# A transformer layer on one core: the second residual, its norm and the Gelu tiles' buffers rebuilt

## The chip, the cores and the metric

One core of one Trainium2 chip runs the whole program in one launch. The time is the device time of the run in microseconds (us). Engines are named as the profile names them: PE is TensorE (matmuls; PEld its weight loads), DVE VectorE, ACT ScalarE, POOL GpSimd, SP SyncE. SP, ACT and POOL also issue DMAs, each into a queue of its own, and every engine works through its own instructions in order.

## The reference

One layer on 512 tokens of width 2048, all in float32: two attention branches, a layer norm, and a PEER block, a retrieval of experts of which 16 out of 16384 are chosen in each of 8 heads. The change touches what stands around PEER:

```
y   = (sigmoid(gate_a) * ya + sigmoid(gate_b) * yb) @ w_o
x   = layer_norm(alpha * x + g1 * y, ln1_g, ln1_b)          # LN1
h2  = x * (1 + sc2) + sh2
p   = peer(h2, ...)
x   = layer_norm(alpha * x + g2 * p, ln2_g, ln2_b)          # the end

def peer: for each token t and head h
    q = h2 @ wq;  top 16 of the scores -> 16 experts e, gates gt
    a = <h2, u_tab[e]>;  w = gt * gelu(a);  p += w * v_tab[e]
```

## The kernel before

**Two ways through PEER.** 352 of the 512 tokens (TD) go the dense way: all 16384 experts are multiplied, as 128 tiles of 128 experts, in 32 groups of four (GE). A u product (u_mm, 96 matmuls of 352 columns) gives a Gelu tile; the tile is multiplied by its gates (weigh), split into a high and a low half (W_0h, W_0l and so on), and goes as moving operand into the v product (v_mm, four blocks of 12 matmuls of 352 columns). The sums of the v products are kept transposed in SBUF, in accT. For the other 160 tokens each chosen row of u_tab and v_tab is gathered from memory (320 indirect DMAs, issued by POOL) and used by DVE.

**Weights.** A Stream (L60 to L100) loads pieces of 128x1024 through SP's queue (raw), ACT rounds each to its high half (whi, L91), DVE takes the difference (wlo, L92). A product takes three matmuls: L151, L154, L155 in the helper mm3; L1141 to L1143 in v_mm.

**Stages, as the trace shows them.** To 1105: conditioning and attention. 1105 to 1340: the product with w_o and LN1, whose normalised rows (rx) POOL stores to n_d (L803). 1340 to 1684: queries, scores against the keys (loaded by POOL, L933) and their top 16, and meanwhile the first 23 u products through u_first (L900). 1684 to 2060, the g phase: for each of 11 chunks of 32 tokens the gates are spread into a tile over all experts, by one-hot rows (o, L1076, DVE), scaled ones (og, L1082, ACT) and their product (L1083, PE); ACT stores 2 MB of them to g_d (L1087), and beside it run three more u products and five gathers. 2060 to 3150, the main loop: 18 groups, u product and v product of the group before, by turns, with gathers paced by step(). 3150 to the end: the 14 groups whose Gelu tiles u_first had stored to ga_d come back (L1252) and only v products remain.

**First Gelu tiles.** u_first's tile glf has one buffer, and its store to ga_d is issued by POOL (L904), in whose queue the gathers and the copies that pace them (L288) stand too.

**The end.** step(VW) paces gathers through the first VN = 9 end groups. After that POOL computes alpha*LN1 again from n_d, by mul_add (L1206 multiplies, L1208 adds, on 512 columns at a time), also for the gathered tokens (h2g, accg) and the 32 mixed ones (accx). In group 12 accT is transposed back by PE (L1280), multiplied by the row g2 on DVE (L1240, yt) and added by POOL (L1241). In group 13 the v products are made with tokens on the partitions (v_part, 128x512 results in PSUM banks), and again yt, add and bn_stats (L1243). finish() (L1217) then makes the norm: for some columns by ACT (L1222) and POOL, for others by DVE (L1227), and stores the result.

**What sets the order.** The functions write instructions in program order for each engine; a scheduler then moves them within what the data and the buffers allow. Pinned ones keep their order (SP's loads, wlo).

## Time and profile before

| | us |
|---|---|
| three timed runs | 3712.43, 3717.99 (median), 3718.40 |
| profiled execution | 3710.02 |
| its span | 3708.2 |
| PE busy in it | 3572.1 (96%) |
| DVE, ACT, POOL busy | 2718.9, 1756.2, 1071.9 |
| granted TensorE clock, mean | 0.985 |

Read it in this way: where one engine is busy nearly throughout, the stages in which it is not are looked up (busy time by stretch), then what it waited for there (waits by releaser), then what the releaser itself did at that moment (timeline of that engine). The rows stand below.

### The profile page before, as it was taken

What the parts mean: (1) busy time and instruction counts of PE and PEld (TensorE: products, weight loads), DVE (VectorE), ACT (ScalarE), POOL (GpSimd) and SP (SyncE); (2) the same over time, 40 slices, a digit from 0 to 9 for tenths busy, and PEclk for the clock granted to TensorE, in tenths of its full rate; (3) what the DMA queues carried; (4) which work ended last, traced back from release to release, by engine and by line L of the source; (5) the groups of instructions that cost most, each with busy time, mean ns of one, the idle gap of its engine ahead of it and who ended that gap; (6) DMA issues with size and microseconds to landing.
All of it is one profiled execution on the core that took longest, in us unless ns stands there. A gap on an engine that the chain in (4) does not pass through costs nothing.

```text
span 3708.2 us, 52907 instructions
## 1 busy us (share of the span) xinstructions
PE 3572.1 (96%) x20073; PEld 3287.0 (89%) x20073; DVE 2718.9 (73%) x3735; ACT 1756.2 (47%) x3055; POOL 1071.9 (29%) x1186
## 2 busy tenths in 40 slices
PE   8999999999999999999998899999999999999977
PEld 6888888877778899899988899999999999899976
DVE  8756587445455669988978587777777778788866
ACT  3233332233333555446755355555455555676652
POOL 0001110011110000004434353433344434345474
PEclk9999999999999999999999999999999999999988
DMA  9645588644365665348988799989898999999942
GB/s 397 248 170 216 176 317 303 233 137 133 121 223 182 200 203 172 121 131 292 356 316 339 278 358 347 338 328 349 329 363 329 347 345 347 367 371 368 359 157 84
DMA packets 211024, 996.73 MB, mean 269 GB/s; under 512 B 26624, under 2 KB 26800, under 8 KB 153648
## 3 DMA queue, kind: packets, MB, share of 16 engines
q1 hardware_dynamic: 132048, 526.45, 40.0%
q0 software_dynamic: 75984, 441.58, 31.8%
q10 hardware_dynamic: 2736, 25.32, 1.7%
q8 instruction: 157, 2.57, 0.3%
q14 instruction: 99, 0.81, 0.1%
HBM read 930.42 MB, written 61.51 MB: 267 GB/s over the span
## 4 chain that ended last, share of the span: by engine, by line
PE 80%; issue 5%; DMA 5%; DVE 5%; POOL 2%; ACT 2%; POOLq 0%; SPq 0%; DVEq 0%; ACTq 0%
PE main L155 11%; PE main L151 11%; PE main L154 11%; PE o L1143 8%; PE o L1141 7%; PE o L1142 7%; PE q L151 6%; PE q L155 6%; PE q L154 6%; DMA adaw<-in_w_ada_t 2%; DVE wlo L92 1%; DMA ga_d<-glf 1%; DVE adaw L292 1%; PE g L1083 1%; DMA row<-in_peer_u,gidx 1%
## 5 line engine op out<-in xcount | busy, mean ns | idle before, releaser
L92 DVE TENSOR_TENSOR wlo<-raw,whi 128x1024 fp32r<-128x1024 f32 x800 | 991.7, 1248 | 558.1 <-ACT whi L91 426.6
L91 ACT ACTIVATE whi<-raw 128x1024 fp32r<-128x1024 f32 x800 | 837.8, 1056 | 941.3 <-PE main L154 489.9
L151 PE MATMUL q<-dh,whi 128*128 128x352 f32 x1680 | 549.4, 327 | 25.5 <-ACT glf L903 24.2
L155 PE MATMUL q<-dh,wlo 128*128 128x352 f32 x1680 | 543.6, 324 | 0.9 <-DVE wlo L92 0.9
L154 PE MATMUL q<-dl,whi 128*128 128x352 f32 x1680 | 543.0, 323 | 0.0
L288 POOL COPY row<-wlo 128x1 f32<-128x1 f32 x320 | 186.7, 584 | 748.7 <-DVE row L1035 322.8
L151 PE MATMUL main<-hh,whi 128*128 128x512 f32 x912 | 352.9, 393 | 9.1 <-ACT hh L346 8.8
L1144 ACT ACTIVATE accT<-o 128x352 f32<-128x352 f32 x496 | 223.7, 462 | 282.5 <-PE o L1143 281.5
L154 PE MATMUL main<-hl,whi 128*128 128x512 f32 x912 | 357.0, 391 | 0.0
L155 PE MATMUL main<-hh,wlo 128*128 128x512 f32 x912 | 349.3, 393 | 0.2 <-DVE wlo L92 0.2
L151 PEld LDWEIGHTS q<-dh,whi 128*128 128x128 f32 x1680 | 318.3, 189 | 27.5 <-ACT glf L903 25.6
L155 PEld LDWEIGHTS q<-dh,wlo 128*128 128x128 f32 x1680 | 318.4, 190 | 1.2 <-DVE wlo L92 1.2
L154 PEld LDWEIGHTS q<-dl,whi 128*128 128x128 f32 x1680 | 319.2, 190 | 0.0
L1035 DVE SCALAR_TENSOR_TENSOR row<-row,h2g 128x2048 f32<-128x2048 f32 x128 | 291.7, 2285 | 29.0 <-DMA row<-in_peer_u,gidx 27.9
L1041 DVE SCALAR_TENSOR_TENSOR h2g<-row,au,h2g 128x2048 f32<-128x2048 f32 x127 | 297.9, 2346 | 8.3 <-DMA row<-in_peer_v,gidx 7.9
L292 DVE SCALAR_TENSOR_TENSOR adaw<-adaw,cond 128x2048 f32<-128x2048 f32 x96 | 218.5, 2288 | 103.9 <-DMA adaw<-in_w_ada_t 100.3
L151 PE MATMUL main<-qh,whi 128*128 128x352 f32 (+2 forms) x752 | 242.2, 323 | 1.0 <-ACT whi L91 1.0
L155 PE MATMUL main<-qh,wlo 128*128 128x352 f32 (+2 forms) x752 | 242.8, 324 | 0.0
L154 PE MATMUL main<-ql,whi 128*128 128x352 f32 (+2 forms) x752 | 242.0, 322 | 0.0
L1060 POOL DMA_INDIRECT row<-in_peer_v,gidx x128 | 217.3, 1698 | 46.7 <-POOL row L288 35.3
L1134 ACT ACTIVATE o<-accT 128x352 f32<-128x352 f32 x480 | 219.2, 471 | 7.4
L151 PEld LDWEIGHTS main<-hh,whi 128*128 128x128 f32 x912 | 172.1, 189 | 46.6 <-ACT hh L346 10.7
(1355 smaller groups left out, 8161.3 us busy)
## 6 DMA issues: line engine op xcount, KB each, us to landing
raw<-in_wst SPq DMA_DIRECT2D x288, 512.0 KB, 3.8
raw<-in_u_t SPq DMA_DIRECT2D x256, 512.0 KB, 6.0
raw<-in_v_t SPq DMA_DIRECT2D x256, 512.0 KB, 7.6
adaw<-in_w_ada_t SPq DMA_DIRECT2D x96, 1024.0 KB, 7.0
g_d<-stg ACTq DMA_DIRECT2D x11, 2048.0 KB, 10.9
gt<-g_d POOLq DMA_DIRECT2D x18, 704.0 KB, 10.4
ga_d<-glf POOLq DMA_DIRECT2D x56, 176.0 KB, 4.4
gl<-ga_d POOLq DMA_DIRECT2D x56, 176.0 KB, 7.9
```

Source lines behind the costliest of these rows:

```text
L91: self.nc.scalar.activation(hi, raw, AF.Copy)
L92: self.pin(self.nc.vector.tensor_tensor(out=lo, in0=raw, in1=hi.bitcast(F32), op=ALU.subtract))
L151: op = nc.tensor.matmul(ps, lh, rh, start=first, stop=False)
L154: nc.tensor.matmul(ps, lh, rl, start=False, stop=False)
L155: nc.tensor.matmul(ps, ll, rh, start=False, stop=last)
L292: pin(nc.vector.scalar_tensor_tensor(w, w, 1.0, cond, op0=ALU.mult, op1=ALU.mult, accum_out=mod[:, j : j + 1]))
L1035: op = nc.vector.scalar_tensor_tensor(row, row, 1.0, h_, op0=ALU.mult, op1=ALU.mult, accum_out=a_[:, c : c + 1])
L1041: op = nc.vector.scalar_tensor_tensor(accs[n], row, a_[:, c : c + 1], accs[n], op0=ALU.mult, op1=ALU.add)
L1141: nc.tensor.matmul(o, vh[:, s], wh, start=first, stop=False, **kw)
L1142: nc.tensor.matmul(o, vh[:, s], wl, start=False, stop=False, **kw)
L1143: nc.tensor.matmul(o, vl[:, s], wh, start=False, stop=last_, **kw)
L1144: nc.scalar.activation(sum_, o, AF.Copy)
```

## The change

1. **LN1** (x1_rows): DVE makes alpha*LN1 with its gain and bias at once, 16 chunks of 128x512 in two buffers (xc), two operations each, and POOL stores each chunk to n_d (256 KB). The four 1 MB stores of the bare normalised rows go.
2. **First Gelu tiles**: glf has two buffers; the store to ga_d is issued by ACT instead of POOL.
3. **g2 upstream**: the last group's eight weight pieces are multiplied by g2 on DVE before they are split (Stream.by); accT is scaled by the g2 column when ACT evacuates it in group 12; accx is multiplied once.
4. **Residual and sums in PSUM**: in the last group ACT writes x1 into a bank, PE adds accT by a matmul with the identity (48 in all, in place of 48 transposes) and the mixed tokens by the selection matrix, and the v products accumulate on top. bn_stats and the norm read the bank.
5. **Gathered tokens** (gathered()): on DVE at group 11 instead of POOL.
6. **Pacing**: VN 9 to 11, VW 1.0 to 0.8; four gl buffers instead of two in the end; six matmuls of 160 columns at group 0 write the rest of each bank.
7. **Norm of the three dense token tiles**: per tile DVE takes columns 512 to 2047, ACT and POOL the first 512.

```diff
@@ Stream.fill
+            by = self.by.get(self.plan[i][0])
+            if by is not None:
+                r2 = raw.rearrange("p (a b) -> p a b", a=2)
+                self.nc.vector.tensor_tensor(
+                    out=r2, in0=r2, in1=by.unsqueeze(1).to_broadcast([P, 2, 512]), op=ALU.mult
+                )
@@ LN1
-        for t in tt:
-            nc.gpsimd.dma_start(n1_d[t], rx[t])
+    def x1_rows(pas):
+        for t in (2 * pas, 2 * pas + 1):
+            for c in range(4):
+                cs = slice(c * 512, (c + 1) * 512)
+                xc = rp_.tile([P, 512], F32, tag="xc", name=f"xc{t}{c}", bufs=2)
+                nc.vector.tensor_tensor(out=xc, in0=rx[t][:, cs], in1=l1["ln1_g"][:, cs], op=ALU.mult)
+                nc.vector.tensor_tensor(out=xc, in0=xc, in1=l1["ln1_b"][:, cs], op=ALU.add)
+                nc.gpsimd.dma_start(n1_d[t][:, cs], xc)
@@ u_first
-        gl = wk.tile([P, TD], F32, tag="gl", name=f"glf{e}", bufs=1)
+        gl = wk.tile([P, TD], F32, tag="gl", name=f"glf{e}", bufs=2)
         nc.scalar.activation(gl, ps[:, :TD], AF.Gelu)
-        nc.gpsimd.dma_start(ga_d[e], gl)
+        nc.scalar.dma_start(ga_d[e], gl)
@@ v_mm
-            nc.scalar.activation(sum_, o, AF.Copy)
+            if by is None:
+                nc.scalar.activation(sum_, o, AF.Copy)
+            else:
+                nc.scalar.activation(sum_, o, AF.Copy, scale=by[:, j * 4 + dd : j * 4 + dd + 1])
@@ pacing
-    VW, VN = 1.0, 9
+    VW, VN = 0.8, NF // GE - 3
     rate = (NROW - RG * NCH) / (2.0 * GE * len(gorder) + VW * GE * VN - 2)
@@ the end
+        st.by = {("v", last, j, x): g2[:, cols(j)] for j in range(4) for x in range(2)}
+        def norm_rows(r, c, src, mv):
+            nc.vector.scalar_tensor_tensor(src, src, mv[:, 0:1], l2g[:, c], op0=ALU.subtract, op1=ALU.mult)
+            nc.vector.scalar_tensor_tensor(r[:, c], src, mv[:, 2:3], l2b[:, c], op0=ALU.mult, op1=ALU.add)
+        def start_sum(t, j):
+            o = o_bank()
+            nc.scalar.activation(o, x1[t][:, cols(j)], AF.Copy)
+            kw = dict(start=False, stop=False, skip_group_check=True)
+            if t == ND - 1:
+                nc.tensor.matmul(o, sel, accx[:, cols(j)], **kw)
+            for dd in range(4):
+                ts_ = slice(t * P, t * P + rows_of(t))
+                nc.tensor.matmul(o[: rows_of(t), dd * P : (dd + 1) * P], accT[:, j * 4 + dd, ts_], ident, **kw)
+            return o
...
+            os_ = {j: start_sum(t, j) for j in (2, 3)}
             for j in (2, 3):
-                os_[j] = o_bank()
                 for x in range(GE):
                     v_part(os_[j], last, x, t, vs[j, x // 2], True)
+                nc.vector.bn_stats(stts[t][:, j, :], os_[j])
+            r, mv = x1[t], moments(wk, stts[t], f"fmv{t}")
+            cs = cols(0)
+            nc.scalar.activation(r[:, cs], r[:, cs], AF.Identity, scale=mv[:, 2:3], bias=mv[:, 3:4])
+            nc.gpsimd.tensor_tensor(out=r[:, cs], in0=r[:, cs], in1=l2g[:, cs], op=ALU.mult)
+            nc.gpsimd.tensor_tensor(out=r[:, cs], in0=r[:, cs], in1=l2b[:, cs], op=ALU.add)
             for j in (2, 3):
-                add_in(t, j, os_[j], nc.vector, 1)
-            finish(t, x1[t], stts[t], nc.scalar if t % 2 else nc.sync, NV[t])
+                norm_rows(r, cols(j), os_[j], mv)
+            store(t, r, cols(2, 2), nc.sync)
+            norm_rows(r, cols(1), r[:, cols(1)], mv)
+            store(t, r, cols(0, 2), nc.scalar)
```

Three places show how the order moves; in the changed kernel the line numbers are some 8 to 30 higher.

PE, late in the g phase, before: q is a u product (left out are 46 more of its matmuls), g the product of a one-hot tile with its scaled one.

```order
9002 L1083 MATMUL g_16702<-o_16704,og 128x128 x4
9003 L1083 MATMUL g_16717<-o_16719,og 128x128 x4
9004 L151 MATMUL q_16512<-dh,whi_16281 128x352
9005 L154 MATMUL q_16512<-dl,whi_16281 128x352
...
9051 L155 MATMUL q_16512<-dh,wlo_16446 128x352
9052 L1083 MATMUL g_16732<-o_16734,og 128x128 x4
9053 L1083 MATMUL g_16747<-o_16749,og 128x128 x4
9054 L151 MATMUL q_16584<-dh,whi_16475 128x352
```

The same place of the changed kernel (there the lines of a u product are L159, L162, L163, and the one-hot product is L1106):

```order
9300 L162 MATMUL q_17178<-dl,whi_16985 128x352
9301 L163 MATMUL q_17178<-dh,wlo_16986 128x352
9302 L1106 MATMUL g_17117<-o_17119,og 128x128 x4
9303 L159 MATMUL q_17246<-dh,whi_17015 128x352
9304 L162 MATMUL q_17246<-dl,whi_17015 128x352
9305 L163 MATMUL q_17246<-dh,wlo_17016 128x352
9306 L1106 MATMUL g_17132<-o_17134,og 128x128 x4
9307 L159 MATMUL q_17246<-dh,whi_17015 128x352
```

The one-hot products, which stood four tiles in a row between whole u products, now mostly stand one by one within them, at 4 and some 24 rows' distance.

POOL, from LN1 to the first loads of the keys, before: n_d takes the normalised rows, h_d and h2x_d the input of PEER.

```order
277 L803 DMA n_d_156<-rx_8760 128x2048
278 L803 DMA n_d_157<-rx_8761 128x2048
279 L933 DMA keys<-in_keys_t 128x128
280 L904 DMA ga_d_162<-glf_11204 128x352
281 L863 DMA h_d<-h2gt 128x2048
282 L870 DMA h2x_d<-h2x 32x2048
283 L933 DMA keys<-in_keys_t 128x128
```

After:

```order
284 L739 TENSOR_TENSOR mv_10302<-mv_10302,mhalf 128x1
285 L824 DMA n_d_156<-xc_10855 128x512
...
292 L824 DMA n_d_157<-xc_10883 128x512
293 L886 DMA h_d<-h2gt 128x2048
294 L893 DMA h2x_d<-h2x 32x2048
295 L956 DMA keys<-in_keys_t 128x128 x16
296 L1027 DMA gx_d<-G 32x128
```

The first load of the keys, which stood right behind the n_d stores, and the second, behind h2x_d, now both stand with the other 14 behind h_d and h2x_d; the stores of Gelu tiles that stood between them are no longer on this engine.

POOL, the last rows of the program before; x_0 to x_2 are the three dense token tiles, yt a product with g2, fmv a mean and its power.

```order
1128 L1241 TENSOR_TENSOR x_2_32643<-x_2_32643,yt_33174 96x512
1129 L731 TENSOR_TENSOR fmv_33214<-fmv_33214,mhalf 128x1
1130 L1206 TENSOR_TENSOR x_0_32021<-x_0_32021,rb 128x512 x3
1131 L1208 TENSOR_TENSOR x_0_32021<-x_0_32021,rb 128x512
1132 L731 TENSOR_TENSOR fmv_33262<-fmv_33262,mhalf 128x1
1133 L1208 TENSOR_TENSOR x_0_32021<-x_0_32021,rb 128x512 x2
1134 L1206 TENSOR_TENSOR x_1_32332<-x_1_32332,rb 128x512
1135 L731 TENSOR_TENSOR fmv_33310<-fmv_33310,mhalf 128x1
1136 L1208 TENSOR_TENSOR x_1_32332<-x_1_32332,rb 128x512
1137 L1206 TENSOR_TENSOR x_2_32643<-x_2_32643,rb 128x512
1138 L1208 TENSOR_TENSOR x_2_32643<-x_2_32643,rb 128x512
```

After; here L1324 and L1325 are the multiply and the add of the norm:

```order
1033 L1238 DMA x_3_32347<-n_d_157 128x2048
...
1036 L1238 DMA x_2_32373<-n_d_156 128x2048
1037 L739 TENSOR_TENSOR fmv_32357<-fmv_32357,mhalf 128x1
1038 L739 TENSOR_TENSOR fmv_33161<-fmv_33161,mhalf 128x1
1039 L1324 TENSOR_TENSOR x_0_32369<-x_0_32369,rb 128x512
1040 L1325 TENSOR_TENSOR x_0_32369<-x_0_32369,rb 128x512
1041 L739 TENSOR_TENSOR fmv_33213<-fmv_33213,mhalf 128x1
1042 L1324 TENSOR_TENSOR x_1_32371<-x_1_32371,rb 128x512
1043 L1325 TENSOR_TENSOR x_1_32371<-x_1_32371,rb 128x512
...
1046 L1325 TENSOR_TENSOR x_2_32373<-x_2_32373,rb 128x512
```

The adds of yt and one multiply and add each are gone: per token tile one power, one multiply and one add are left on POOL, in that order.

## Rows read from the trace of the kernel before

**Rows 1.** The page, parts 1 and 5 (busy us, mean ns of one).

```profile
PE 3572.1 (96%) x20073; PEld 3287.0 (89%) x20073; DVE 2718.9 (73%) x3735; ACT 1756.2 (47%) x3055; POOL 1071.9 (29%) x1186
...
L92 DVE TENSOR_TENSOR wlo<-raw,whi 128x1024 fp32r<-128x1024 f32 x800 | 991.7, 1248 | 558.1 <-ACT whi L91 426.6
```

**Rows 2.** Waits of PE, whole span: engine line, waited for, total us, times, longest.

```profile
PE q L151 <- ACT glf L903: 24.2, 6, 15.0
PE o L1143 <- DVE wlo L92: 19.4, 15, 8.2
...
PE o L1142 <- DVE W_2l L245: 7.3, 2, 7.0
```

**Rows 3.** Stretches: length, busy (PE, PEld, DVE, ACT, POOL), granted clock, DMA share, GB/s.

```profile
1105.00:1340.00 235.00, 234.46 (x1233) 197.80 (x1234) 143.17 (x186) 112.64 (x143) 5.88 (x9) 1.00 0.63 204
...
1684.00:2060.00 376.00, 340.90 (x2274) 336.52 (x2272) 299.16 (x342) 227.86 (x531) 153.73 (x148) 0.97 0.87 328
2060.00:3150.00 1090.00, 1080.42 (x6728) 1076.69 (x6729) 850.84 (x737) 561.36 (x951) 457.22 (x431) 1.00 0.90 339
3150.00:3500.00 350.00, 333.24 (x2016) 323.39 (x2016) 284.24 (x233) 236.69 (x466) 169.01 (x181) 1.00 0.96 367
3500.00:3647.00 147.00, 125.06 (x721) 120.93 (x720) 100.80 (x84) 83.34 (x158) 92.22 (x77) 0.91 0.55 187
...
3682.00:3708.00 26.00, 0.00 (x0) 0.00 (x0) 16.48 (x23) 1.63 (x2) 17.76 (x12) 0.54 0.30 121
```

**Rows 4.** Groups by line, 1680 to 2070: busy, mean, idle before, releaser.

```profile
L1035 DVE SCALAR_TENSOR_TENSOR row<-row,h2g 128x2048 f32<-128x2048 f32 x53 | 120.9, 2284 | 23.2 <-DMA row<-in_peer_u,gidx 22.1 <-POOL row L288 1.1
...
L903 ACT ACTIVATE glf<-q 128x352 f32<-128x352 f32 x33 | 15.0, 455 | 42.6 <-DMA ga_d<-glf 41.0 <-PE g L1083 1.2 <-ACT stg L1084 0.4
```

**Rows 5.** DMA issues, 1680 to 2070: count, KB each, median us to landing.

```profile
ga_d<-glf POOLq DMA_DIRECT2D x33, 176.0 KB, 7.6
```

**Rows 6.** Timeline of ACT's queue, fifth store of g_d: start us, us.

```profile
1825.97 0.33 ACTq L1087 DMA_DIRECT2D g_d<-stg  x1
```

**Rows 7.** That line's own view: ns min/median/max, first and last start; landings.

```profile
L1087 ACTq DMA_DIRECT2D g_d<-stg x11: 326/327/337, 1707.7 to 2022.8; - x11
...
DMA to landing us min/median/max: 7.4/10.9/14.2
```

**Rows 8.** Timeline of DVE, 3515 to 3568: start us, us, idle before.

```profile
3520.17 8.33 DVE L1115 TENSOR_TENSOR gl<-gl,ra 128x352 f32<-128x352 f32 x2
...
3543.52 15.83 DVE L92 TENSOR_TENSOR wlo<-raw,whi 128x1024 fp32r<-128x1024 f32 x3 [10.33 <-ACT whi L91]
3559.27 0.94 DVE L1115 TENSOR_TENSOR gl<-gl,rb 128x352 f32<-128x352 f32 x2
```

**Rows 9.** Timeline of POOL, the same stretch.

```profile
3544.82 5.03 POOL L1206 TENSOR_TENSOR x<-x,ra 128x512 f32<-128x512 f32 x4
```

**Rows 10.** Timeline of POOL after the last matmul.

```profile
3681.48 6.96 POOL L1206 TENSOR_TENSOR x<-x,rb 128x512 f32<-128x512 f32 x3 [2.03 <-ACT x L1222]
...
3701.45 1.59 POOL L1208 TENSOR_TENSOR x<-x,rb 128x512 f32<-128x512 f32 x1
```

**Rows 11.** Timeline of DVE in the same stretch.

```profile
3683.44 2.06 DVE L1227 SCALAR_TENSOR_TENSOR x<-x,fmv,rb 128x512 f32<-128x512 f32 x3
```

**Rows 12.** Timeline of PE: one-hot products (1699.77) and transposes (3619.87), start and length.

```profile
1699.77 1.50 PE L1083 MATMUL g<-o,og 128*128 128x128 f32 x12
...
3619.87 0.60 PE L1280 MATMUL q<-ident,accT 128*128 128x128 f32 x4
```

**Rows 13.** Timeline of POOL around the first loads of the keys.

```profile
1320.13 0.56 POOL L933 DMA_DIRECT2D keys<-in_keys_t  x1
...
1363.48 0.52 POOL L870 DMA_DIRECT2D h2x_d<-h2x  x1 [6.04 <-ACT h2x L869]
```

**Rows 14.** DMA issues, 1345 to 1380: count, KB each, median us to landing.

```profile
h2x_d<-h2x POOLq DMA_DIRECT2D x1, 256.0 KB, 3.0
keys<-in_keys_t POOLq DMA_DIRECT2D x2, 64.0 KB, 3.5
```

More of the change, by code (lines that the diff above doesn't have):

```diff
@@ L1153, in v_part @@
         s = slice(x % 2 * 512, (x % 2 + 1) * 512)
-        mm3(o[: rows_of(t)], (wh[:, ts_], wl[:, ts_]), (v[0][:, s], v[1][:, s]), x == 0, x == GE - 1, keep)
+        for i, (l, r) in enumerate(((wh, v[0]), (wl, v[0]), (wh, v[1]))):
+            op = nc.tensor.matmul(
+                o[: rows_of(t)], l[:, ts_], r[:, s], start=False, stop=x == GE - 1 and i == 2,
+                skip_group_check=True,
+            )
+            if keep and i == 0:
+                tc.keep_in_program_order(op)
     pace = [0.0]
@@ L1200, in tile_encoder_layer @@
             )
-        def mul_add(r, m, s, chunks):
-            for c in chunks:
-                cs = slice(c * 512, (c + 1) * 512)
-                nc.gpsimd.tensor_tensor(out=r[:, cs], in0=r[:, cs], in1=m[:, cs], op=ALU.mult)
-                if s is not None:
-                    nc.gpsimd.tensor_tensor(out=r[:, cs], in0=r[:, cs], in1=s[:, cs], op=ALU.add)
-        def base(t):
-            x1 = gr.tile([P, D], F32, tag="row", name=f"x1_{t}")
-            nc.gpsimd.dma_start(x1, n1_d[t])
-            mul_add(x1, rows["ln1_g"], rows["ln1_b"], range(4))
-            return x1
@@ L1254, in tile_encoder_layer @@
             if g == VN:
                 gather(NROW)
[L1256 to L1270 removed]
+                gathered()
```

117 lines of the change are left out of this document (51 added, 66 removed).

## The prediction

> **What bounds the kernel now.** I read the page first: TensorE (PE) is busy 96% of the span [rows 1]. So the time is PE's work plus the places where PE stands still, and an edit is worth only what it takes out of those places, or what it adds to PE. The second view is the waits of PE, summed by releaser [rows 2]: 24.2 us for a Gelu (L903), 19.4 us for the low half of a weight piece (wlo, VectorE, DVE) and 7.3 us for the low half of a weighed Gelu tile (W_2l). The third places them [rows 3]. PE is idle 35.1 us in the g phase (376 less 340.9), 9.6 us in the 1090 us of the main loop, 16.8 us in the first 350 us of the end, 21.9 us in the next 147 us; after 3682 it does nothing for the last 26 us, which is pure tail. The granted clock also falls under 1.00 in the g phase (0.97) and in 3500 to 3647 (0.91). The level below full is half (1.2 of 2.4 GHz), so 0.97 of 376 is some 11 us of lost work, and 0.91 of 147 up to 13 us. Both are stages with long stops of PE; in stages without one the clock is 1.00. A stop so costs more than itself.
>
> **The change part by part**, against the profiled execution: 3710.02 us, span 3708.2. That run lies 8.0 us under the median of the three timed ones (3717.99) and 2.4 under the lowest, so the predicted time gets 2 us on top of the sum.
>
> *Gelu tile in two buffers, its store on ScalarE's (ACT) queue.* With one buffer the Gelu of tile e waits until the store of tile e-1 has landed: ACT stood 41.0 us for that [rows 4], and a store lands 7.6 us after its issue [rows 5]. With two it waits for e-2. What is late next? DVE's load is 299 us of 376 [rows 3]; the DMA engines are busy 0.87 of it. Neither is full, but neither leaves much: at the share of 0.96 that they reach in 3150 to 3500, the same bytes need 376 x 0.87/0.96 = 341 us. The first chunks show what the phase can do: g_d is stored first at 1707.7 and, four chunks later, at 1825.97, 29.6 us a chunk; the eleventh and last store is at 2022.8, so the other six took 32.8 each [rows 6, 7]. So 23.7 us to the first store, ten chunks of 29.6 and about 24 us for the last three Gelu tiles give 344 us against 376: -32. Ends: -15 if the transfers or DVE hold half of it, -42 if the half-clock stretches go as well. The order helps: the one-hot matmuls are now spread among the u matmuls late in the phase too, where before they stood in bunches.
>
> *Fewer POOL steps in the queue.* POOL loses 33 Gelu stores, each of which held the gathers behind it while it waited for the Gelu; ACT gains them. A store issue holds ACT for about what g_d's took, 0.33 us [rows 7], 11 us in 376 with ACT busy 228 [rows 3]: nothing on the path.
>
> *Gathers spread over 11 end groups at weight 0.8 instead of 9 at 1.0.* The rate goes from 265/178 to 265/177.2 per step, so in the end 1.20 gathers per v_mm instead of 1.49, over 44 v_mm's. Where the 16.8 us of idle of 3150 to 3500 stand, the DMA share is 0.96 [rows 3]; a fifth fewer bytes by gather eases DVE and DMA alike. I take -8, half of it (0 to -15).
>
> *End of the POOL passes.* Before, x1 is rebuilt in the end by POOL multiplies and adds (L1206, L1208). While they run, the pair of weighings at L1115 takes 8.33 us where the same pair takes 0.94 afterwards, and three wlo, of 1.25 us each on average [rows 1], take 15.83 us [rows 8], while POOL works at four multiplies for 5.03 us and then at adds [rows 9]. Right behind them PE has its longest stops of the end, 7.0 us for W_2l and 8.2 us for wlo [rows 2]. After, x1 comes ready from the LN1 stage, and the passes on accg and accx are 5 DVE operations of 1024 or 2048 columns plus 8 norm operations of 1024, some 15 us of DVE at L1035's 2.3 us per 2048 columns [rows 4]. Also new on DVE: 8 multiplications of a weight piece by g2, about as long as a wlo of the same shape, 10 us, in 80 us of the last two groups; DVE was busy 100.8 of 147 us, and loses the 24 yt products and their adds. Of the 21.9 us of idle and some 9 of half clock I take -20 (-8 if the new DVE work stands ahead of a wlo in its turn, -28 if all goes).
> The Trainium skill, "SBUF — State Buffer", section "SBUF: two separate sides", says that a DVE operation with two SBUF inputs and a GpSimd operation that reads SBUF take one port pair in turns, the loser blocking for the whole instruction. The rows just cited agree in that one DVE operation outlasts several POOL ones. By it the term would be -28, not -20, since what blocks is then gone entirely.
>
> *Tail.* After the last matmul: 26.5 us, in which POOL works 6.96 us on three multiplies and its last add ends at 3703 [rows 10]; the span ends 5 us later, with the last store. After, for the last tile: statistics and their aggregate, 1 us, three DVE operations of 0.7 (three took 2.06 [rows 11]), ACT 0.7, two POOL operations of 1.6 [rows 10] while DVE does three more: about 7 us, then 5 us for the last store as now. 12 against 26.5: -14.5 (-11 if POOL's two operations take 2.3 each, as those of the 6.96 us row, and DVE waits with them; -17 if the column done by POOL ends with DVE's own).
>
> *PE work added.* 48 accT matmuls by the identity replace 48 transposes. A transpose is one row of 0.11 us (four in 0.60), an fp32 product is two rows of 0.11 each (twelve rows in 1.50) [rows 12], so 0.11 more each: +5.5, and the six small ones of 160 columns +0.5. The selection matmuls stay. +6.
>
> *x1 at LN1.* 32 DVE operations of 128x512 at 0.7 us [rows 11], 22 us, in a stage of 235 us in which DVE is busy 143 and PE 234.5 [rows 3]; and 16 stores of 256 KB in place of four of 1 MB. A store of that size lands 3.0 us after its issue [rows 14]. With two buffers a chunk takes (1.4 + 3.0)/2 = 2.2 us, 17 us for the eight of a pass, between which DVE has weight pieces to split: DVE, which works in order, holds those up by at most 0.8 us a chunk while it waits for a buffer. Cover: the pieces split ahead. If it were gone, 22 us of work and 13 of waiting stand before PE, of which DVE's 92 idle us of the stage take most. I take +1 (0 to +8).
>
> *Keys behind the stores.* On POOL the first load of the keys stood ahead of the h2 stores and was issued at 1320.13; the second, behind the h2x store of 1363.48 [rows 13]. Now all 16 stand behind both stores, while PE goes to the first right after h2x. One issue and one landing (0.5 + 3.5 [rows 13, 14]) and the first product after it: +5 (0 if PE has other matmuls in between, +8 if two are waited for).
>
> *Order of the main loop.* The v and u pieces alternate unevenly from its start, as they do before only in the later half of the loop, whose idle in all is 9.6 us [rows 3]: +4 (0 to +10, as much again).
>
> Sum: -32 - 8 - 20 - 14.5 + 6 + 1 + 5 + 4 = -58.5, so 3651.5, and with the 2 us **3653**. Ends: all good ends -42-15-28-17+6 = -96 (3616), all bad ends -15-0-8-11+6+8+8+10 = -2 (3710).
>
> **The rivals.** *The g phase stays at its transfers.* If the gathers, now freed from waiting behind Gelu stores, run earlier and collide with the weight loads, the phase gives 10, not 32, and the end nothing: 3653 + 22 + 8 = 3683. For it: 341 us at the highest share of any stage is already the forecast's own 344. Against: 29.6 us a chunk was kept up for four chunks.
> *The Gelu store gets stuck behind g_d: slower.* On ACT's queue the 176 KB store follows the 2 MB g_d store (10.9 us to landing, at most 14.2 [rows 7]). If it lands only after that one, 10.9 + 7.6 = 18.5 us. Two buffers allow two periods, 2 x 29.6/3 = 19.7 us. Beyond that ACT, which works in order, blocks the Gelu and all one-hot scalings and splits behind it, once per chunk: 11 us for each us. The saving of 58.5 is eaten at 19.7 + 58.5/11 = 25.0 us; if the store waits out its own landing at the slowest and one of g_d's, 2 x 14.2 = 28.4 us, it costs 11 x 8.7 = 96 us: 3653 + 96 = 3749.
> The Trainium skill, "DMA: Bandwidth & Descriptors", section "Queues, rings and completion order", says that each queue row has its own ring per DMA engine and that an engine takes turns between rows by packet. By it a store on ACT's row waits for what is left of g_d but no longer for POOL's gathers, which share POOL's: by it the landing is nearer to the forecast's than to this rival's.
> *The waits move, only the tail gains.* The waits for weight pieces (wlo) come from late raw pieces; then only the tail (-14.5) and part of the Gelu term (-15) stay, against +16: 3698.
>
> **How the numbers follow.** Forecast 0.68 (3653, 3620 to 3675); g phase stays at its transfers 0.15 (3683); waits move 0.10 (3698, half of whose cases lie above 3700); stuck store or blocked LN1 0.07 (3749). The range is 3615 to 3700: the ends of the sum, cut on the high side where only the last cases lie. 0.2%, 7.4 us, is about what a measurement of this kernel can tell from no change; faster means under 3710.6. The first two cases and most of the third are: 0.89; within 0.2%: 0.05; slower: 0.06.
>
> **What would show it.** PE's wait for glf gone from the list, and the g phase near 344 us at a clock of 1.00; ACT's wait for ga_d near zero (the stuck store would show there, with landings over 20 us). In the last 150 us no stop of 7 or 8 us and no DVE wlo over 2 us. From the last matmul to the end some 12 us. A stop of about 5 us near 1365 for the keys. LN1 still at 100% PE. Wrong would be: a g phase over 365 us, or new idle of over 15 us at LN1 or in the main loop.

## The result and the profile after

| | before | after |
|---|---|---|
| median of 4 runs side by side, us | 3715.21 (3711.6 to 3718.4) | 3651.94 (3650.49 to 3652.83) |
| profiled execution (span), us | 3710.02 (3708.2) | 3652.83 (3650.3) |

The ratio is 0.983 [0.9813, 0.9847]: 63.3 us less by the medians, 57.2 by the two profiled executions. The two figures differ because before's profiled run lies 5.2 us under its median here (the forecast of 3653 had allowed 2) and after's lies 0.9 over. The steps below are read from profile to profile, where the sum of the prediction was -58.5; the results of the experiments are medians.

The page of after shows TensorE (PE) at 98%, where [rows 1] had 96%, and POOL with 159 us less:

```profile
PE 3564.6 (98%) x20127; PEld 3285.3 (90%) x20127; DVE 2700.8 (74%) x3754; ACT 1755.3 (48%) x3072; POOL 912.9 (25%) x1068
```

The waits of PE over the whole span (engine line, waited for, total us, times, longest) answer [rows 2]. The Gelu wait, which was the first row with 24.2 us, is down to 1.3; waits for weight pieces now stand first, and `qs` is new:

```profile
PE o L1166 <- DVE wlo L100: 15.9, 10, 6.1
PE main L159 <- ACT hh L354: 11.2, 3, 8.6
PE o L1164 <- ACT whi L99: 10.7, 9, 2.9
PE main L159 <- ACT qs L950: 7.4, 1, 7.4
...
PE q L159 <- ACT glf L926: 1.3, 1, 1.3
```

The stretches (length, busy of PE, PEld, DVE, ACT, POOL, granted clock, DMA share, GB/s) answer [rows 3]; their borders are moved with the work:

```profile
1105.00:1340.00 235.00, 235.00 (x1242) 199.03 (x1241) 162.59 (x217) 111.99 (x139) 14.89 (x25) 1.00 0.68 222
1340.00:1684.00 344.00, 330.45 (x2020) 310.99 (x2018) 302.68 (x969) 157.64 (x233) 13.49 (x26) 0.98 0.45 145
1684.00:2030.00 346.00, 339.44 (x2303) 338.21 (x2302) 292.78 (x339) 229.21 (x541) 114.04 (x106) 0.98 0.88 335
2030.00:3120.00 1090.00, 1070.11 (x6618) 1063.00 (x6617) 847.93 (x734) 547.73 (x943) 449.07 (x430) 0.99 0.92 342
3120.00:3470.00 350.00, 335.35 (x2047) 329.36 (x2046) 268.32 (x237) 236.75 (x460) 143.49 (x170) 0.99 0.94 347
3470.00:3600.00 130.00, 129.41 (x800) 127.05 (x800) 105.61 (x97) 94.59 (x181) 34.98 (x39) 1.00 0.79 291
```

Three things are seen. The g phase (1684 to 2030) is 30 us shorter and has 6.6 us of idle left where it had 35.1. The end (3470 to 3600) has 0.6 us of idle and the full clock. But the main loop, which lost 9.6 us in 1090, now loses 19.9, and its clock is no longer 1.00.

Stretches with borders set by eye can't be subtracted from each other, so the accounting goes by equal work: I counted PE's matmuls of the u products (u) and of the v products (v) in both traces, 6144 and 5952 of them, took the start of the matmul with the same number in each, and subtracted. (48 such matmuls make one u product, not the 96 of the section on the kernel before, and 48 make one v product.) At u 2816 and at the last u, PE has the same number of matmuls behind it in both. A step is the time that after gained (minus) or lost between two such points.

| from, to (start of the matmul) | before, us | after, us | step |
|---|---|---|---|
| start to first u (through LN1) | 1341.4 | 1337.5 | -3.9 |
| to u 256 (h2 rows, first keys) | 1414.3 | 1418.9 | +8.5 |
| to u 2816 (g phase and the first 128 u behind it) | 2083.1 | 2048.5 | -39.2 |
| to last u, 6144 (main loop) | 3141.0 | 3126.7 | +20.3 |
| to v 3472 | 3188.5 | 3186.2 | +12.0 |
| to v 5208 | 3488.8 | 3470.8 | -15.7 |
| to last v, 5952 (36 of the 48 transposes and 4 selection matmuls moved out of this stretch) | 3646.7 | 3590.9 | -37.8 |
| to last matmul (they and their like, moved in) | 3681.3 | 3638.3 | +12.8 |
| to the end of the span | 3708.2 | 3650.3 | -14.9 |

The tail is the one that was forecast. In the merged timeline of all engines (start us, us, engine, line, operation) from the last matmul on, [rows 10, 11] had three POOL multiplies of 6.96 us and a last add that ended at 3703:

```profile
3638.28 0.40 PE L1181 MATMUL o<-wlo,W_3h 128*96 128x512 f32 x1
3638.72 0.70 DVE L1320 BATCH_NORM_STATS2 stt<-o 128x6 f32<-128x512 f32 x1 [2.08 <-PE o L1181]
...
3643.19 1.50 DVE L1244 SCALAR_TENSOR_TENSOR x<-x,fmv,rb 128x512 f32<-128x512 f32 x1
...
3644.22 1.59 POOL L1325 TENSOR_TENSOR x<-x,rb 128x512 f32<-128x512 f32 x1
3645.84 0.34 ACTq L1247 DMA_DIRECT2D out_dram<-x  x1
```

From the last matmul's start to the last POOL add's end are 7.5 us, then the store: 12 us in all.

The stretch of DVE that answers [rows 8] holds the passes over h2g and h2gx (accg and accx in the code), now on DVE. Three wlo take 3.52 us where they took 15.83:

```profile
3554.58 2.29 DVE L1268 TENSOR_TENSOR h2gx<-h2gx,ra 128x2048 f32<-128x2048 f32 x1
3556.79 3.52 DVE L100 TENSOR_TENSOR wlo<-raw,whi 128x1024 fp32r<-128x1024 f32 x3
...
3561.03 2.35 DVE L1260 TENSOR_TENSOR h2g<-h2g,x 128x1024 f32<-128x1024 f32 x2
```

The stop that the prediction put at the keys came, by another way. Where [rows 13] had the second keys load after the h2x store, the first one is there in POOL's timeline of after. It doesn't wait for the store to be issued but for h_d to land:

```profile
1356.66 0.52 POOL L893 DMA_DIRECT2D h2x_d<-h2x  x1 [2.04 <-ACT h2x L892]
1362.62 0.57 POOL L956 DMA_DIRECT2D keys<-in_keys_t  x1 [5.45 <-DMA h_d<-h2gt]
```

So does ACT's copy of the first queries, for which PE then stands 7.38 us. That is the same releaser, and neither instruction reads h_d:

```profile
1362.42 0.39 ACT L949 ACTIVATE qs<-main 128x256 f32<-128x256 f32 x1 [5.10 <-DMA h_d<-h2gt]
```

### The profile page after: what moved, and what is told of

Same layout as the page of the kernel before. It is cut to its first block, busy times and chain, and to the rows that moved or that the text cites. A ratio compares the mean times of both kernels' runs of the same rounds, so it can differ in the third digit from the quotient of the medians.

```text
span 3650.3 us, 52934 instructions
## 1 busy us (share of the span) xinstructions
PE 3564.6 (98%) x20127; PEld 3285.3 (90%) x20127; DVE 2700.8 (74%) x3754; ACT 1755.3 (48%) x3072; POOL 912.9 (25%) x1068
## 5 line engine op out<-in xcount | busy, mean ns | idle before, releaser
L100 DVE TENSOR_TENSOR wlo<-raw,whi 128x1024 fp32r<-128x1024 f32 x800 | 971.7, 1221 | 543.5 <-ACT whi L99 337.9
L159 PE MATMUL q<-dh,whi 128*128 128x352 f32 x1680 | 546.7, 325 | 2.0 <-ACT glf L926 1.3
L163 PE MATMUL q<-dh,wlo 128*128 128x352 f32 x1680 | 542.5, 324 | 2.1 <-DVE wlo L100 2.0
L162 PE MATMUL q<-dl,whi 128*128 128x352 f32 x1680 | 543.1, 323 | 0.0
L296 POOL COPY row<-wlo 128x1 f32<-128x1 f32 x320 | 167.8, 525 | 896.3 <-DVE row L1058 404.3
L159 PE MATMUL main<-hh,whi 128*128 128x512 f32 x912 | 352.7, 393 | 11.4 <-ACT hh L354 11.2
L162 PE MATMUL main<-hl,whi 128*128 128x512 f32 x912 | 356.4, 391 | 0.0
L163 PE MATMUL main<-hh,wlo 128*128 128x512 f32 x912 | 348.7, 392 | 0.0
L159 PEld LDWEIGHTS q<-dh,whi 128*128 128x128 f32 x1680 | 316.6, 188 | 3.1 <-ACT glf L926 1.6
L163 PEld LDWEIGHTS q<-dh,wlo 128*128 128x128 f32 x1680 | 316.6, 189 | 3.2 <-DVE wlo L100 3.0
L162 PEld LDWEIGHTS q<-dl,whi 128*128 128x128 f32 x1680 | 317.8, 189 | 0.0
L1064 DVE SCALAR_TENSOR_TENSOR h2g<-row,au,h2g 128x2048 f32<-128x2048 f32 x127 | 298.0, 2347 | 6.4 <-DMA row<-in_peer_v,gidx 5.9
L159 PE MATMUL main<-qh,whi 128*128 128x352 f32 (+2 forms) x752 | 242.8, 323 | 7.4 <-ACT qs L950 7.4
L163 PE MATMUL main<-qh,wlo 128*128 128x352 f32 (+2 forms) x752 | 242.7, 323 | 0.0
L162 PE MATMUL main<-ql,whi 128*128 128x352 f32 (+2 forms) x752 | 242.0, 322 | 0.0
L159 PEld LDWEIGHTS main<-hh,whi 128*128 128x128 f32 x912 | 172.1, 189 | 48.8 <-ACT hh L354 12.8
```

Of the source, the lines that this page charges most:

```text
L100: self.pin(self.nc.vector.tensor_tensor(out=lo, in0=raw, in1=hi.bitcast(F32), op=ALU.subtract))
L159: op = nc.tensor.matmul(ps, lh, rh, start=first, stop=False)
L162: nc.tensor.matmul(ps, lh, rl, start=False, stop=False)
L163: nc.tensor.matmul(ps, ll, rh, start=False, stop=last)
L296: eng.tensor_copy(t[:, 0:1], src.bitcast(F32)[:, 0:1])
L1064: op = nc.vector.scalar_tensor_tensor(accs[n], row, a_[:, c : c + 1], accs[n], op0=ALU.mult, op1=ALU.add)
```

## The experiments

Medians are of 4 runs (10 for b_dve). A ratio is against runs of before taken beside them, whose medians lie between 3715.2 and 3717.8; so a difference of a microsecond or two between two versions is not told from none. A name with a_ is an edit of the changed kernel, one with b_ an edit of the kernel before. Of each edit the changed lines are shown, cut where they repeat.

### The Gelu tiles: buffers and queue

Theory: the second buffer gives the g phase, and the queue of the store doesn't matter. Rival: the queue does. The four combinations of one or two buffers with a store on POOL or ACT tell them apart; after is the fourth.

```diff
 a_1buf_pool:
-        gl = wk.tile([P, TD], F32, tag="gl", name=f"glf{e}", bufs=2)
+        gl = wk.tile([P, TD], F32, tag="gl", name=f"glf{e}", bufs=1)
-        nc.scalar.dma_start(ga_d[e], gl)
+        nc.gpsimd.dma_start(ga_d[e], gl)
 a_1buf_act: the first pair alone. a_2buf_pool: the second pair alone.
```

> The changed kernel with the Gelu tiles as before: one buffer, store issued by POOL. The order of the main loop is then regular again in its first half. Theory A (two buffers won 39 us in the g phase, and the uneven order that came with them cost 15 to 20 in the main loop): the g phase takes 376 us again, PE idles little in the first half of the main loop, 3652 + 20 = 3672 us (3665 to 3680). Theory B (the loss in the main loop comes from other parts of the change): 3652 + 39 = 3691.

> The changed kernel with two Gelu buffers, but the store issued by POOL as before. Theory A (the second buffer alone removes the wait): g phase as in the changed kernel within 4 us, PE's wait for glf under 3 us, 3652 (3648 to 3657). Theory B (POOL's queue holds the stores, since gathers and their pacing stand in it, so the landing comes more than two tiles late): the wait for glf stays at 10 us or more, 3665 (3660 to 3672).

> The changed kernel with one Gelu buffer, the store issued by ACT. Theory A (the buffer is what counts): like one buffer with the store on POOL, 3671 (3665 to 3676). Theory B (the queue counts: ACT issues the store right behind the Gelu, POOL some us later): half of the wait for glf goes, 3660 (3654 to 3665). Rival of the prediction (a store behind the 2 MB one blocks ACT): with one buffer it would have to show as stops of over 10 us, 3690 or more.

| median, us (lowest to highest) | store on POOL | store on ACT | ACT costs |
|---|---|---|---|
| one buffer | 3670.73 (3669.51 to 3671.59) | 3679.40 (3677.39 to 3680.14) | +8.7 |
| two buffers | 3643.96 (3641.81 to 3646.96) | 3651.94 (3650.49 to 3652.83) | +8.0 |
| second buffer gives | -26.8 | -27.5 | |

By equal work, against before:

| step, us | 1 buffer, POOL | 1 buffer, ACT | 2 buffers, POOL | 2 buffers, ACT (after) |
|---|---|---|---|---|
| u 256 to u 2816 (g phase) | -3.3 | +4.2 | -50.1 | -39.2 |
| u 2816 to last u (main loop) | +4.4 | +4.5 | +23.6 | +20.3 |

The two halves of the edit add up, and they have opposite signs. The second buffer gives 43 to 47 us in the g phase and loses 16 to 19 of them in the main loop, where the two versions with one buffer lose 4.4 and 4.5. Those 4 are not the price that the prediction put on the uneven order: with one buffer PE's order and SP's loads are as even as in before through the first half of the loop. Where they come from stays open. The ACT queue loses 8 to 11 in the g phase. Runs of neighbouring cells don't overlap (the intervals of the ratios against before do, by up to 0.2%, as before's own runs scatter by 7 to 17 us). The g phase of a_2buf_pool, of the same stretch as in the block of after, is full, at the full clock:

```profile
1684.00:2030.00 346.00, 345.45 (x2375) 345.16 (x2374) 294.38 (x339) 230.62 (x541) 133.14 (x143) 1.00 0.89 342
```

With one buffer and the store on ACT it is the worst of the four:

```profile
1684.00:2030.00 346.00, 324.85 (x2156) 321.94 (x2156) 285.61 (x332) 221.38 (x529) 121.26 (x106) 0.96 0.86 322
```

Landing isn't the reason: the stores land 7.7 us after issue on ACT's queue and 8.5 on POOL's (two buffers, medians of the stretch). What differs is POOL, whose copies ahead of the gathers stand far longer. By lines (busy, mean ns, idle before, releasers), after:

```profile
L296 POOL COPY row<-wlo 128x1 f32<-128x1 f32 x50 | 45.4, 908 | 204.4 <-DVE row L1058 113.5 <-DVE wlo L100 90.8
```

and a_2buf_pool:

```profile
L296 POOL COPY row<-wlo 128x1 f32<-128x1 f32 x51 | 41.5, 815 | 90.5 <-DVE row L1058 76.3 <-DVE wlo L100 14.0
L927 POOL DMA_DIRECT2D ga_d<-glf x33 | 19.3, 585 | 101.4 <-ACT glf L926 101.2 <-issue 0.2
```

With stores on POOL, POOL waits for the Gelu (101.2 us) instead of for a weight split on DVE (14.0 against 90.8). DVE's dots then wait 10.4 us for gathered rows in the stretch, in after 16.8; with one buffer it is 12.6 with stores on POOL and 27.2 with stores on ACT. And what DVE is late with, PE waits for: one-hots stand behind a dot that waits. After has one such stop, in DVE's timeline:

```profile
1816.12 2.29 DVE L1058 SCALAR_TENSOR_TENSOR row<-row,h2g 128x2048 f32<-128x2048 f32 x1 [7.12 <-DMA row<-in_peer_u,gidx]
...
1818.34 0.69 DVE L1099 TENSOR_TENSOR o<-iota,eT 128x512 f32<-128x512 f32 x1
```

and in PE's:

```profile
1819.17 2.05 PE L1106 MATMUL g<-o,og 128*128 128x128 f32 x8 [4.72 <-DVE o L1099]
```

The clock is at its lower level (1.2 of 2.4 GHz) for 6.8 us around its end, 5.8 of them behind it. That ACT's queue costs some 8 us is shown. Why a store less in POOL's queue makes a gathered row come later, whether by where the order puts the gathers or by when POOL is free for them, stays open.

The edit alone in the kernel before:

```diff
-        gl = wk.tile([P, TD], F32, tag="gl", name=f"glf{e}", bufs=1)
+        gl = wk.tile([P, TD], F32, tag="gl", name=f"glf{e}", bufs=2)
-        nc.gpsimd.dma_start(ga_d[e], gl)
+        nc.scalar.dma_start(ga_d[e], gl)
```

> The kernel before with nothing changed but the Gelu tiles: two buffers and the store on ACT's queue. Theory A (this wins 39 us in the g phase and loses some 20 in the main loop because the order there becomes uneven with it): g phase near 338 us, main loop with 20 us of idle, 3715 - 19 = 3696 us (3690 to 3703). Theory B (the loss in the main loop belongs to other parts of the change): 3715 - 39 = 3676.

It ran in 3688.38, against 3717.79 for before: 0.9921 [0.99, 0.9942], between the two. By equal work it gains 41.8 us up to u 2816, and has 19.6 left of that at the last u. So the g phase gains about what after gains there, and the main loop takes back 22, with none of the other edits in. The next stretch takes back more: at v 5208 only 3.6 us are left, in the one profile that there is. With the gathers paced as in before, nearly all of the gain is used up there; a_vn9 (below) points to the pacing as what keeps it in after.

### The main loop

In before, PE runs groups of 48 u and 48 v in turn through the first half of the loop, and SP loads two u pieces and two v pieces in turn. In after both are mixed from its start (behind the first group, PE runs 8 v, 26 u, 35 v, 22 u and on; SP loads one to three pieces of a kind at a time). "Pinned" means that the scheduler may not move an instruction; SP's loads and the wlo splits are pinned in both kernels only up to the start of the attention stage, not here. Theory A: PE's own uneven order makes the stops. Rival: the order of the stream (loads on SP and the splits on DVE) does. a_pin pins PE's order alone; a_st_pin pins also the stream; a_best pins both from the second group on, and h2w as below.

```diff
 a_pin:
+    keep = [False]          (u_mm, v_mm: first matmuls keep program order)
+    keep[0] = True          (main loop)
 a_st_pin, besides:
+    inorder[0] = True       (main loop: loads and splits keep program order)
 a_best:
+            keep[0] = inorder[0] = 1 <= n < len(gorder)
-    with pool("h2w", 1) as wk:
+    with pool("h2w", 1, "right") as wk:
```

> The changed kernel, with the first matmul of every triple of the u and v products in the main loop held in program order, so that 48 u matmuls and 48 v matmuls alternate as they do in the first half of the loop of the kernel before. Theory A (the main loop of the changed kernel loses some 20 us because its u and v products are executed in an uneven order, so that weight pieces are split too late): PE's idle in the loop falls from 20 us to under 5, the first matmul after the g phase is reached at the same time, and the whole takes 3652 - 18 = 3634 us (3628 to 3641). Theory B (the transfers bound the loop: the same bytes now have to come in less time): the order changes nothing, idle stays near 20 us, 3652 (3647 to 3657).

> As a_pin (u and v products of the main loop in program order), and the loads and splits of the weight pieces in the main loop held in program order too, so that the stream runs v v u u as in the first half of the loop before, where a_pin still had v u v u in places on SP, ACT and DVE. Theory A2 (the 20 us of idle come from the stream: a split stands behind a gathered-row dot or behind a piece that PE needs later): the main loop idles under 8 us, 3644 - 15 = 3629 us (3624 to 3636). Theory B (the transfers bound the loop): it stays at 20 us or more of idle, 3644 (3640 to 3650).

> The changed kernel with products and weight stream of the main loop in program order from its second group to its last but one (not in the first group, where the same pin put a weight split behind six gathered-row dots and stopped PE for 11 us at 2051), and with h2gt and h2x on the other side of SBUF. Theory A2 (the uneven stream costs the main loop some 15 us of its 20): loop idle under 10 us and no stop of over 4 us at its start, 3635 - 11 - 3 - 1 = 3620 us (3612 to 3630). Theory B (what is won in the stream is lost at its ends again, where the order is free): 3630 to 3637.

a_pin 3644.39 (0.9808 [0.9792, 0.9824]); a_st_pin 3635.23 (0.9777 [0.9754, 0.9799]); a_best 3637.17 (0.9787 [0.9768, 0.9806]). Of the loop without its first 80 us, 2110 to 3120, the one row of the stretch in before, after, a_pin and a_st_pin, in this order, each from its own trace:

```profile
2110.00:3120.00 1010.00, 1000.42 (x6245) 996.69 (x6244) 792.25 (x679) 529.50 (x905) 424.42 (x396) 1.00 0.91 344
```

```profile
2110.00:3120.00 1010.00, 991.37 (x6131) 984.85 (x6131) 791.76 (x677) 520.50 (x903) 417.63 (x399) 0.99 0.92 343
```

```profile
2110.00:3120.00 1010.00, 992.71 (x6172) 987.82 (x6170) 797.35 (x680) 543.18 (x901) 435.13 (x401) 0.99 0.90 344
```

```profile
2110.00:3120.00 1010.00, 1000.46 (x6243) 994.77 (x6242) 801.76 (x684) 542.30 (x910) 445.61 (x405) 1.00 0.93 349
```

Pinning PE alone leaves the idle at 17.3 us (18.6 in after): theory A falls for the loop, and what a_pin gained came behind it. Pinning the stream as well, which is all that a_st_pin adds, brings the idle back to 9.5, as in before, and the count of matmuls in the stretch with it. The mean share of the transfers isn't at its limit: a_st_pin moves more bytes in the time than after. By equal work, the pieces from u 3328 to the last u take 907.7 us in before, 907.0 in a_st_pin and 909.8 in a_best, but 919.1 in after and 918.4 in a_pin. So it is the uneven order of loads and splits that slows the loop. (The stream was not pinned by itself.)

Pinning has its own price, at its start: a wlo pinned behind dots that wait for gathered rows. In a_st_pin, DVE:

```profile
2047.84 2.29 DVE L1060 SCALAR_TENSOR_TENSOR row<-row,h2g 128x2048 f32<-128x2048 f32 x1 [5.80 <-DMA row<-in_peer_u,gidx]
...
2050.06 2.35 DVE L100 TENSOR_TENSOR wlo<-raw,whi 128x1024 fp32r<-128x1024 f32 x2
```

and PE, whose clock is at the lower level for 13.65 us, 5.8 of them behind the stop:

```profile
2051.33 0.66 PE L163 MATMUL q<-dh,wlo 128*128 128x352 f32 x1 [11.15 <-DVE wlo L100]
```

a_best was to avoid that stop and met a longer one where its pin begins (16.58 us at 2086.58). Both versions beat before and after; they can't be told apart. The stops also leave something open: a_st_pin comes out of its stop 14.1 us later than after (at u 2816), a_best 12.4 (at u 3328), and no version that was run has its last u before 3117.6. So whether the even order would keep its rate if the loop began as early as in after isn't shown. A store on POOL (a_2buf_pool) together with a pinned stream was not run.

### The keys

Theory: the copies and the first keys load get memory that h2gt, whose store is under way, has just left; the pools laid out differently, the stop goes. The rival: the keys' own place in POOL's queue takes its place.

```diff
-    with pool("h2w", 1) as wk:
+    with pool("h2w", 1, "right") as wk:
```

> The changed kernel, with the buffers of the transposed PEER input (h2gt, h2x) on the other side of SBUF, so that the buffers of the keys and of the scores no longer take the place from which h_d and h2x_d are still being stored. The order of POOL stays as it is. Theory A (the 7.4 us stop of PE at 1363 waits for those two stores to land because the memory is reused): the stop and the half clock behind it go, 3652 - 9 = 3643 us. Theory B (as in the prediction: the keys stand behind the stores in POOL's queue, and that is what costs): the stop stays at 4 us or more, 3652 - 0 to 4.

> Both edits of the two runs before together. If the losses are independent (different stages, each a stop of PE) the gains add: 3652 - 18 - 9 = 3625 us (3617 to 3634). If the transfers bound the main loop, what is won ahead of it is given back there: 3643 or more.

a_h2w ran in 3650.68 (0.9828 [0.9812, 0.9845]), 1.3 under after, which the runs can't tell from none. The wait for the landing is gone; POOL issues the load at once:

```profile
1357.20 0.52 POOL L893 DMA_DIRECT2D h2x_d<-h2x  x1 [2.04 <-ACT h2x L892]
1357.71 0.57 POOL L956 DMA_DIRECT2D keys<-in_keys_t  x1
```

PE's stop for qs goes from 7.38 to 2.15, but 7 us later PE stands 3.80 us for the keys themselves:

```profile
1365.34 2.05 PE L960 MATMUL tp<-keys,qs 128*128 128x128 f32 x8 [3.80 <-DMA keys<-in_keys_t]
```

So both are right: the shared memory was the wait that ended last, and the place behind the stores the next one. (ACT's first Gelu tile now waits 6.26 us for h2x_d to land; PE doesn't wait for it there.) With PE's order pinned as in a_pin besides, a_pin_h2w ran in 3641.61 (0.9802 [0.9786, 0.9819]), 10 under after; the 3625 that the expectation's sum gave rested on a_pin's own -18, which didn't come either; nor did a_h2w's -9.

### The end: which engine, and how much work

Theory: the stretching of DVE beside POOL ([rows 8, 9]) was the cost in before. Rival: it is the amount of work ahead of PE's next piece. a_gpool puts after's five passes on POOL; b_dve takes before's rebuilding of x1 from POOL to DVE.

```diff
 a_gpool (all five passes over accg and accx):
-                nc.vector.tensor_tensor(out=accg[:, cs], in0=accg[:, cs], in1=g2[:, cs], op=ALU.mult)
+                nc.gpsimd.tensor_tensor(out=accg[:, cs], in0=accg[:, cs], in1=g2[:, cs], op=ALU.mult)
 b_dve (multiply and add of mul_add, but the last tiles' finish):
-                nc.gpsimd.tensor_tensor(out=r[:, cs], in0=r[:, cs], in1=m[:, cs], op=ALU.mult)
+                eng.tensor_tensor(out=r[:, cs], in0=r[:, cs], in1=m[:, cs], op=ALU.mult)
```

> The changed kernel, with the multiplications by g2 and the additions on accg and accx (five operations of 1024 or 2048 columns) on POOL instead of DVE; the norm of the gathered tokens stays on DVE. Theory A (POOL passes over SBUF stretch DVE's two-input operations while they run, so that weight splits come late, as in the kernel before): splits and weighings of 4 us or more appear between 3540 and 3600, PE stops for 5 us or more there, 3652 + 10 = 3662 us (3656 to 3672). Theory B (the amount of work was the problem, and moving 10 us of it off DVE relieves DVE): 3652 or up to 3 us less.

> The kernel before, with its multiplies and adds that rebuild x1 and scale accg and accx on DVE instead of POOL (44 operations of 128x512, some 30 us more for DVE, which was busy 101 of 147 us); the norm at the very end stays as it is. Theory A (the stops of 7 and 8 us were POOL and DVE stretching each other): they go although DVE has more to do, 3715 - 15 = 3700 us (3692 to 3708). Theory B (the amount of DVE and POOL work in these 147 us): DVE now stands ahead of its splits for longer, 3715 + 0 to 15.

a_gpool ran in 3653.85 (0.9832 [0.9812, 0.9852]), 1.9 over after. The stretching is back in full. DVE and then POOL:

```profile
3554.80 11.58 DVE L100 TENSOR_TENSOR wlo<-raw,whi 128x1024 fp32r<-128x1024 f32 x3 [0.89 <-ACT whi L99]
```

```profile
3554.00 4.64 POOL L1268 TENSOR_TENSOR h2gx<-h2gx,ra 128x2048 f32<-128x2048 f32 x1 [6.19 <-DVE h2gx L1064]
...
3559.20 6.11 POOL L1260 TENSOR_TENSOR h2g<-h2g,x 128x1024 f32<-128x1024 f32 x2
```

Three splits take 11.58 us instead of 3.52. But PE pays one stop of 1.7 us for a wlo, and the 1.9 us by the medians can't be told from none: the splits come early enough. So the stretching by itself does not cost what [rows 8] seemed to show, where there is little else.

b_dve ran in 3705.82, against 3717.79 for before, 12 less by the medians; by the interval of the ratio, 0.9974 [0.9963, 0.9986], it is 5 to 14. By equal work it loses 6.3 us from v 3472 to v 5208 and gains 13.7 from there to the last v. Up to 3560 no row of its end is stretched, and of 21.9 us of idle [rows 3] 12.0 are left:

```profile
3500.00:3647.00 147.00, 135.05 (x797) 130.49 (x796) 105.44 (x131) 90.54 (x172) 42.13 (x42) 0.94 0.57 197
```

What is left are stops for the weighings, which now stand behind DVE's own row of x1 work:

```profile
PE o L1141 <- ACT W_2h L253: 7.1, 1, 7.1
PE o L1142 <- DVE W_2l L245: 2.9, 1, 2.9
```

From 3514 up to these weighings DVE works without a gap, most of it the passes over x1, accg and accx. The edit left the norm of the gathered tokens on POOL, and beside that DVE's rows are stretched again (DVE and then POOL; an L245 takes 0.52 us otherwise). PE doesn't stop there:

```profile
3568.91 4.82 DVE L245 TENSOR_TENSOR W_3l<-gl,W_3h 128x352 fp32r<-128x352 f32 x1
```

```profile
3560.03 5.63 POOL L1207 TENSOR_TENSOR h2g<-h2g,rb 128x512 f32<-128x512 f32 x4 [0.26 <-ACT h2g L1223]
```

So of the 21.9 us of idle some 10 went with the stretching and some 12 stay with the amount of work. The split is rough: b_dve also puts some 30 us of work on DVE, so it shows a net. In after the idle of both kinds is gone; x1 is made at LN1 there, but most of the other edits bear on the end too, and what each is worth was not taken apart.

### The pacing of the gathers

```diff
-    VW, VN = 0.8, NF // GE - 3
+    VW, VN = 1.0, 9
```

> The changed kernel with the gathers paced as before: over 9 end groups with weight 1.0, and the gathered tokens' sums at group 9. Theory A (the term of -8 us in the prediction: fewer gathers per v product ease the first 350 us of the end): 3652 + 8 = 3660 us (3655 to 3667). Theory B (those stops came from elsewhere): 3652 (3648 to 3655).

The edit also moves the sums of the gathered tokens from group 11 to group 9, which begins at v 5184. It ran in 3670.20 (0.9867 [0.9851, 0.9884]): 18.3 over after, more than either theory had it. The loss lies between v 3472 and v 5208: a_vn9 is 2.5 us ahead of after at the first and 19.9 behind at the second. The stretch, to be held against 335.35 us and 143.49 of POOL in after:

```profile
3120.00:3470.00 350.00, 329.34 (x1988) 319.57 (x1987) 275.67 (x238) 228.63 (x446) 169.77 (x179) 0.99 0.95 354
```

PE's waits from 3120 on have many short stops for pieces, ten for whi against four in after, and eight for wlo against two:

```profile
PE o L1164 <- ACT whi L99: 12.6, 10, 2.9
PE o L1166 <- DVE wlo L100: 5.9, 8, 1.1
```

## Why the prediction came out, term by term

The forecast of 3653 met 3651.9, but that is partly luck of sums. Against the steps of the first table:

- **Gelu tiles, -32: -39.2.** The reading was right: the wait for glf is gone (1.3). The clock came back only in part: between u 256 and u 2816 PE works 22.6 us at the lower level in before and 11.5 in after. Nor was it worth the 11 us that the prediction took from 0.97 of 376: of the 24.8 us at that level PE stood still in 13.7. The term was too small all the same: at a share of 0.89 the transfers still kept PE full in a_2buf_pool.
- **Stores from POOL to ACT, "nothing on the path": +8.0 to +8.7.** A wrong step. I asked what ACT pays for an issue, and not what POOL does when it no longer waits for the Gelu: it runs into the waits on DVE instead. With the store left on POOL the phase gives 50.1.
- **Main loop, +4 (0 to +10): +20.3.** The step that failed. I had seen the uneven order and priced it by the idle of before's later half, "as much again". The versions with the second buffer and no pins have that order from the start of the loop and lose 20 to 24 us; those with one buffer are even there and lose 4. PE's idle grew by 10.3 us (19.9 less 9.6), already the top of the range. Another 4 us or so is the clock: PE works 11.7 us at the lower level in the loop of after and 3.4 in before's. The prediction's own first paragraph says that a stop costs more than itself, and this term left that out. The rest, some 6 us, no row explains. a_pin and a_st_pin show that the order of loads and splits is what costs, and not that of the matmuls.
- **Keys, +5 (0 to +8): +8.5.** Right in place and sign. The stop is 7.4 us for another reason (memory still being stored), and the lower clock that begins within it lasts 4.5 us beyond it. Without the first reason the one that was named takes over (a_h2w).
- **LN1, +1: -3.9.** The stage stays at 235.00 of 235; x1 shows no cost there. The -3.9 itself says little: before, b_dve and b_2buf_act, the same up to there, reach the first u at 1341.4, 1342.9 and 1346.6.
- **Pacing, -8: +12.0 and -15.7, together -3.7.** Two things in one place. a_vn9, with the old pacing, loses 11.9 over the same two stretches; against that the new pacing gives 15.6 by the profiles and 18 by the medians, twice the term. What the forecast lacked is that the rest of the change costs 12 here. b_2buf_act loses 15.9 here with the second buffer and its store alone: the old pacing seems to hold PE up more when it comes earlier. Of the new pacing's own, the +12.0 holds a stop of 6.1 us at 3163, with the clock low for 6.2 us behind it; a_vn9 has 2.9 in its place, so the stop goes with the pacing. It doesn't go with the uneven order: the one-buffer versions have it too (6.1). Where products are pinned the stops there are others (2.3 us in a_pin, 8.5 in a_st_pin, none over 1 in a_best). In the timelines of after, the weighted sums of gathered rows (L1064) stand before the wlo on DVE:

```profile
3156.48 4.74 DVE L1064 SCALAR_TENSOR_TENSOR h2g<-row,au,h2g 128x2048 f32<-128x2048 f32 x2
3162.35 1.23 DVE L100 TENSOR_TENSOR wlo<-raw,whi 128x1024 fp32r<-128x1024 f32 x1 [1.12 <-POOL row L296]
```

```profile
3163.63 0.66 PE L1166 MATMUL o<-W_0h,wlo 128*128 128x352 f32 x1 [6.14 <-DVE wlo L100]
```

- **End of the POOL passes and the PE work added, -20 + 6 = -14: -37.8 + 12.8 = -25.** Sign and place were right; the size was beyond the good end of -22, since almost nothing is left: 0.6 us of idle, clock 1.00. The reason was half right. b_dve splits the gain: some 10 us of the idle went with the sharing between POOL and DVE, some 12 stayed with the amount of work, and a_gpool has the same stretching at a cost that the runs can't tell from none. The new work was counted too high besides: the norm of the gathered tokens is four operations of 1024 columns, not eight. By the Trainium skill, "SBUF — State Buffer", section "SBUF: two separate sides", the prediction had -28 instead of -20, which with the +6 is -22 and lies nearer. The trace agrees with its rule in that DVE's splits are stretched while POOL's operations run (11.58 us for three), but the rule doesn't say what that costs PE.
- **Tail, -14.5: -14.9.** Right, step for step.

The +6 for PE's own work can be read by itself. The 48 accT products by the identity are 96 rows in the trace, which start 0.11 us apart, as the prediction had it from [rows 12]; 8 of them, with the end of the last:

```profile
3632.07 1.04 PE L1281 MATMUL o<-ident,accT 128*96 128x128 f32 x8
```

Of the rivals, the stuck store didn't happen: the view of the store's own line shows that no store took over 15.7 us to land, where the rival began at 19.7 us and 18.5 was its starting point.

```profile
DMA to landing us min/median/max: 1.8/4.2/15.7
```

"The g phase stays at its transfers" fell with -39. "The waits move" was half right: waits for weight pieces did move, into the main loop (+20.3) and to 3163 (+12.0), but after v 5208 they went for good. So the total was met because the g phase, the POOL passes and LN1 came out 7, 11 and 5 us better than forecast, and the main loop, the keys and the first part of the end 16, 3.5 and 4 worse. That these cancel is luck.

## What to carry to other kernels

When an edit ends a stall, look at the order that it leaves for the next stage: here the second buffer was worth over 40 us in its own stage and gave up 16 to 19 of them in the loop behind it, because loads and splits no longer came in an even order. An instruction that is moved off a queue also takes its waiting off that queue, and that waiting may have kept others in step; cost both queues, not only the one that gains. And two engines that slow each other are worth fixing only as far as the slower one's results are waited for: three splits stretched to 15.8 us held PE for 8.2 us in before, and three stretched to 11.6 us held it for 1.7 in a_gpool.
